# Hybrid encoder block on one core: y tiles loaded two gelus ahead, rope tables, loads and stores on other queues, PSUM pools in another order, and the out-projection by token tile

## The chip, the cores and the metric

The kernel runs on one core of one Trainium2 chip. The metric is the device time of one execution in microseconds (us). An execution is described by one profiled run: its trace has every instruction of TensorE (PE, with its weight loads PEld), VectorE (DVE), ScalarE (ACT) and GpSimd (POOL), and the DMA issues of SyncE (SP), ACT and POOL.

## What is computed

One layer of a bidirectional encoder on 256 "prompt" and 512 "sample" tokens of width 1024, all in float32. The two groups share the weights and do not see each other.

```python
h = rmsnorm(x, norm_mix_g)
u, q, k, v, qm, gl = split(h @ w_in)
# A: S5, a diagonal complex state space in both directions
y = s5_direction(u, ...) + flip(s5_direction(flip(u), ...)) + s5_d * u
z = gelu(y)
s5_out = z * sigmoid(z @ s5_w_glu)
# B: differential attention, 8 heads, two softmax maps per head
q, k = rope(rmsnorm(q, q_g)), rope(rmsnorm(k, k_g))
a = softmax(q1 k1) - lam * softmax(q2 k2)
diff_out = rmsnorm(a @ v, sub_g) * (1 - lambda_init)
# C: attention into 256 memory tokens, 4 heads
mem_out = memory_attention(qm, rmsnorm(mem, mem_norm_g), w_mem_kv, ...)
merged = sum(sigmoid(gl + b_gate)[n] * (branch[n] @ w_branch[n]) for n in 3)
x = x + merged @ w_out
h2 = rmsnorm(x, ffn_norm_g)
g, up = split(h2 @ w_gate_up)
x = x + (silu(g) * up) @ w_down
```

`lam` is exp(lq1·lk1) − exp(lq2·lk2) + a constant.

## The kernel before

**Precision.** Every float32 operand of a dense product is split into a high part (`...hi`, `wh`) and a low part (`...lo`, `wl`), and each product is three matmuls, hi·hi, hi·lo and lo·hi (`mm3`, lines 752 to 754). So nearly all PE rows of the profile have these three lines; the tile's name tells the stage.

**Weights.** `WStream` brings the weights in two pieces of 128x1024 each: an SP DMA into `wr` (line 539, three buffers), an ACT copy that makes `wh` (line 596), and `wl` by a DVE subtraction (line 602) or, with `by_dma`, by an ACT copy of the negated piece (line 599) and a POOL DMA that adds `wr` in flight (line 600). `wh` and `wl` have four buffers each. `get()` hands out a weight and prepares the next one.

**Tiles and order.** There are 768 tokens, six tiles of 128; many matmuls take them as segments of 256 and 512 (`SEGS`). The tile framework's scheduler orders the instructions of each engine; the source feeds it generators that a `Pace` object ticks at chosen rates, so that the dense matmuls of one stage are mixed with small operations of another. Each engine executes its own list in order. PSUM has eight banks, shared out by `psum(stage, d, a, b, wide)` to four kinds of tiles ("d" for dense products, "a", "b", and a double bank "w").

**Stages**, with the times of the profiled run:

- 0 to 270: memory keys, values and queries, norms, memory attention. Its output goes through `mo` tiles to `mo_scr` in DRAM.
- 270 to 628: S5. Its parameters, then the gate logits `gl` (12 weights) mixed with sixteen S5 steps. Each step ends in `psY` matmuls and an ACT copy `Ysb` (line 443) that is stored to `y_scr`; DVE's rotated input is `X` (line 390). Pools: d 2, b 4, w 1.
- 628 to 921: differential attention's projections. Pools anew: d 3, a 2, b 3. First the rope tables: twelve POOL operations (lines 1091 to 1099), and on DVE and ACT the sum and exp of `lam` (lines 1104 to 1109; the exp is line 1107). Then 72 units of 24 matmuls, 256 columns each: six `qk` units per head (ACT copy and square, lines 1125 and 1127) or six `v` units per pair of heads (ACT copy to `V`, line 1157). At units 2, 4, ..., 16 one `gelu(m)` is emitted: eight SP DMAs load a tile `y` with a reshuffle from `y_scr` (line 451), ACT squares (`yt`, line 1312) and takes tanh (line 1314), DVE does the rest (lines 1313 and 1316), SP stores `zz` to `z_scr` (line 1319). `y` has one buffer. After unit 16 (`DIFF_START`), each unit also ticks the attention `dat`: `stack` transposes q and k, copies them to `kst`/`qst` (ACT, line 1179) and swaps halves by a POOL DMA (`kst<-kst`, line 1187); `scores` does `sc` (lines 1220 and 1221), the maximum on DVE (line 1226) and exp on ACT (`p`, line 1228); then `aT`, `av` and the store of a head to `br_scr` by SP.
- 921 to 1034: branch 2 (memory), with the attention's rest ticked between its matmuls; its inputs `xm` come by 16 POOL DMAs (line 1470).
- 1034 to 1237: the GLU product with `zs` loads from `z_scr`, then branches 0 and 1. Each branch tile M loads a gate `glr` (line 1440, two buffers, SP), takes tanh on ACT (line 1441) and multiplies and adds on DVE (lines 1446 and 1449). `brr` and `x1` loads are on SP too.
- 1237 to 1305: out-projection `wo`. Pools anew: d 6, b 2. Four weights, column half c times input half kh, and for each all six token tiles (`out_rows`); the kh = 1 half adds to `x1` (line 1531).
- 1305 to 1357: row norms (`nxn`, line 793), transposes `nT` (line 781) with evacuations `fhi` and `flo` (line 746), the first gate and up products.
- 1357 to 1823: the FFN in blocks of 256 hidden columns, seven products each for gate and up instead of eight (sums of weight quarters `ws` on POOL), and `dn`, twelve tiles a block, which alternate between "b" and "d" banks and are added to x by DVE (line 1417).

Of the kernel before, what the change touches and what calls it, by code (L numbers as in the profile page):

```python
# [491 lines left out]
MEM_RATE = 1.2  # L492
DIFF_TAIL = 1.8
DIFF_RATE = 6.0 / 9.0
DIFF_START = 16
DIFF_HEADS = (0, None, 1, 2, None, 3, 4, None, 5, 6, 7, None)


# [4 lines left out]
class WStream:  # L503
# [97 lines left out]
            return  # L601
        self.sub.tensor_tensor(out=lo, in0=r, in1=hi.bitcast(F32), op=ALU.subtract)  # L602

    def ahead(self, i, parts=True):
        n = 2 * len(self.src)
        while self.n_dma < min(n, 2 * i + 3):
            self._dma()
        while parts and self.n_split < min(n, 2 * i + 2):
            self._split()
            if self.n_dma < min(n, self.n_split + 3):  # L610
                self._dma()

    def get(self):
        i = self.next
        self.next += 1
        self.ahead(i + 1)
        _, kk, cols, kind = self.src[i]
        p = self.parts.pop(i)
        if kind == "w":
            return p  # L620
        k2 = kk // 2
        at = lambda t, k, c0, n: t[:, cols * (k % k2) + c0 : cols * (k % k2) + c0 + n]
        return lambda k, c0, n: tuple(at(t, k, c0, n) for t in p[k // k2])


def hybrid_block(ctx, tc, A, outs, consts):
# [24 lines left out]

    PS, pctx = {}, [ExitStack()]

    def psum(stage, d, a, b, wide=0):
        pctx[0].close()
        pctx[0] = ctx.enter_context(ExitStack())
        for k, n in (("d", d), ("a", a), ("b", b), ("w", wide)):
            if n:
                PS[k] = pctx[0].enter_context(tc.tile_pool(name=f"ps{k}{stage}", bufs=n, space=PSUM))

    psum(0, 3, 2, 3)
    psd = lambda n="d": PS["d"].tile([128, 512], F32, name=uid(n), tag="d")
    env.psa = lambda n="a": PS["a"].tile([128, 512], F32, name=uid(n), tag="a")
    env.psb = lambda n="b": PS["b"].tile([128, 512], F32, name=uid(n), tag="b")
# [219 lines left out]
    def mem_attend():  # L884

        for h in range(4):
# [14 lines left out]
            for i in range(TILES + 2):  # L901
                if i in (3, 7):
                    sg = 0 if i == 3 else 1
                    c0, n = SEGS[sg]
                    for e in range(2):
                        mo = [k2.tile([128, 512], F32R, name=uid("mo" + w), tag="mo" + w, bufs=1) for w in "hl"]
                        ps = env.psb("mo")
                        es = slice(128 * e, 128 * e + 128)
                        for c in range(2):
                            mm3(ps[:, 0:n], vv[0][:, 2 * sg + c, es], vv[1][:, 2 * sg + c, es],  # L910
                                PT[0][:, c, 0:n], PT[1][:, c, 0:n], c == 0, c == 1)
                        split_evac(mo[0][:, 0:n], mo[1][:, 0:n], ps[:, 0:n])
                        for w in range(2):
                            nc.sync.dma_start(mo_scr[w][2 * h + e][:, c0 : c0 + n], mo[w][:, 0:n].bitcast(F32))
# [37 lines left out]
    with tc.tile_pool(name="nrm", bufs=1) as pool, tc.tile_pool(name="nrmg", bufs=1) as pg:  # L952
        xm = [load_rows(pool, ms[0])]
        gm = bcast_load(pg, A["mem_norm_g"][0], 1024, "gmem")
        xm += [load_rows(pool, ms[tt]) for tt in range(1, 4)]
        W.ahead(0, parts=False)
# [89 lines left out]

    with ExitStack() as c2:
        s5.open_work(c2)
        psum(1, 2, 0, 4, 1)
        glp = c2.enter_context(tc.tile_pool(name="glp", bufs=2))  # L1050
        pace = Pace(s5.steps(y_scr), S5_RATE)
        for c in range(12):
            W.by_dma = True
            w = W.get()
            for m in range(2):
                M = 2 * c + m
                for sg, (c0, n) in enumerate(SEGS):
                    gt = glp.tile([128, 512], F32, name=uid("glt"), tag="glt")
                    ps = psd("gl")
                    dense_fm(ps, w, m, H, c0, n)  # L1060
                    act.activation(gt[:, 0:n], ps[:, 0:n], AF.Identity, bias=bg[:, M : M + 1])
                    nc.sync.dma_start(gl_scr[M][:, c0 : c0 + n], gt[:, 0:n])
                    pace.tick(1.0 + sg)
        pace.drain()
    psum(2, 3, 2, 3)
    s5ctx.close()


# [14 lines left out]
    for i, nme in enumerate(("diff_q_g", "diff_k_g")):  # L1083
        g = rp[:, 2, 64 * i : 64 * i + 64]
        nc.sync.dma_start(g, A[nme][0].unsqueeze(0).to_broadcast([128, 64]))
        bc = lambda a: a.unsqueeze(2).to_broadcast([128, 4, 2, 32])
        cos, sin = bc(tab[:, :, 0:32]), bc(tab[:, :, 32:64])
        gb = lambda a: a.unsqueeze(1).unsqueeze(1).to_broadcast([128, 4, 2, 32])
        g1, g2 = gb(g[:, 0:32]), gb(g[:, 32:64])
        s_ = slice(2 * i, 2 * i + 2)  # L1090
        gp.tensor_tensor(out=tC[:, :, s_, 0:32], in0=cos, in1=g1, op=mul)
        gp.tensor_tensor(out=tC[:, :, s_, 32:64], in0=cos, in1=g2, op=mul)
        gp.tensor_tensor(out=tS[:, :, s_, 0:32], in0=sin, in1=g2, op=mul)
        gp.tensor_tensor(out=tS[:, :, s_, 32:64], in0=sin, in1=g1, op=mul)
        if i == 0:

            for t in (tC, tS):
                gp.tensor_scalar(out=t[:, :, s_], in0=t[:, :, s_], scalar1=0.125, scalar2=None, op0=mul)
        gp.tensor_scalar(out=tS[:, :, s_, 0:32], in0=tS[:, :, s_, 0:32], scalar1=-1.0, scalar2=None, op0=mul)
# [93 lines left out]
    def diff_attend():  # L1193
# [79 lines left out]
        def finish(h):  # L1273
            osb = X.pop(("h", h))[0]
            do = stg.tile([128, TOK], F32, name=uid("do"), tag="do", bufs=1)
            for t0, t1 in ((0, 2), (2, 6)):
                ps = env.psb("oT")
                for t in range(t0, t1):
                    pe.transpose(ps[:, 128 * (t - t0) : 128 * (t - t0) + 128], osb[:, t], env.ident)
                act.activation(do[:, 128 * t0 : 128 * t1], ps[:, 0 : 128 * (t1 - t0)], AF.Copy, scale=subg)  # L1280
            nc.sync.dma_start(br_scr[h], do)

        for i in range(N + 5):
            h, tt = divmod(i, TILES)
# [16 lines left out]
                finish(h - 1)  # L1301
            yield


    def gelu(m, pool):
        C0 = math.sqrt(2.0 / math.pi)
        y = pool.tile([128, 8, 97], F32, name=uid("y"), tag="y")
        t = pool.tile([128, 8, 97], F32, name=uid("yt"), tag="yt")
        z = stg.tile([128, TOK], F32, name=uid("zz"), tag="brr")
        s5.load_y(y, y_scr[m])  # L1310
        f = lambda a: a.rearrange("p i k -> p (i k)")
        act.activation(f(t), f(y), AF.Square)
        v.scalar_tensor_tensor(out=f(t), in0=f(t), scalar=1.0 / 0.044715, in1=f(y), op0=add, op1=mul)
# [7 lines left out]
    dat = Pace(diff_attend(), DIFF_RATE)  # L1321
    n_unit = 0
    with tc.tile_pool(name="gelu", bufs=1) as yp:
        for h in DIFF_HEADS:
            if h is not None:
                last = h
            for u_ in (v_units(last // 2) if h is None else qk_units(h)):
                n_unit += 1
                if n_unit % 2 == 0 and n_unit <= 16:
                    gelu(n_unit // 2 - 1, yp)  # L1330
                if n_unit > DIFF_START:
                    dat.tick()
    W.by_dma = False
# [30 lines left out]
    def first(what, sg, m):  # L1364


        if what not in fw:
            new_block(what, 0)
            fw[what] = W.get()
        c0, n = SEGS[sg]  # L1370
        ps = psd(what)
        dense_fm(ps, fw[what], m, F, c0, n)
# [49 lines left out]
    with ExitStack() as c5:  # L1422
# [9 lines left out]
        def branch(n_, X, first=False, MG=None, tick=lambda w: None, hook=None):  # L1432
            for c in range(4):
# [3 lines left out]
                for m in range(2):  # L1437
                    M = 2 * c + m
                    g = gtp.tile([128, TOK], F32, name=uid("glr"), tag="glr")
                    nc.sync.dma_start(g, gl_scr[8 * n_ + M])  # L1440
                    act.activation(g, g, AF.Tanh, scale=0.5)
                    for sg, (c0, n) in enumerate(SEGS):
                        ps = psd("br")
# [16 lines left out]
        def load_pair(X, src, scale=None, more=()):  # L1460
            for m in range(8):
                p = zst if m in more else stg
                r = p.tile([128, TOK], F32, name=uid("brr"), tag="brr")
                nc.sync.dma_start(r, src[m])
                split_evac(X[0][:, m], X[1][:, m], r, scale)

        Xm = pair(XA, "xm")
# [21 lines left out]
        for c in range(4):  # L1489
            w = W.get()  # L1490
            for m in range(2):
                M = 2 * c + m
                t = gtp.tile([128, TOK], F32, name=uid("gt"), tag="glr")
                zs = stg.tile([128, TOK], F32, name=uid("zs"), tag="brr")
                nc.sync.dma_start(zs, z_scr[M])
                for c0, n in SEGS:
                    ps = psd("glu")
                    dense_fm(ps, w, m, Z, c0, n)
# [75 lines left out]
    def right_factors():  # L1574

        with tc.tile_pool(name="ffb", bufs=1, side="right") as p:
# [1 line left out]
            hs = [slice(2 * j, 2 * j + 2) for j in range(2)]  # L1578

            def whole(t, b, j=slice(0, 4)):  # L1580
                v.tensor_tensor(out=t, in0=B[b][0][:, j].bitcast(F32), in1=B[b][1][:, j].bitcast(F32), op=add)
                return t

            def parts(n_):
# [84 lines left out]
```

## Time and profile before

| | us |
|---|---|
| median of 3 runs | 1828.95 (1828.82 to 1829.65) |
| the profiled execution | 1828.94 |
| its span in the trace | 1827.2 |
| PE busy (98% of the span) | 1782.8 |
| DVE busy (71%) | 1290.9 |
| ACT busy (48%) | 878.9 |
| POOL busy (14%) | 254.6 |

The mean granted clock of PE is 0.992 of full speed. In a table by windows each row is a stretch of the span: the busy time and number of instructions of PE, PEld, DVE, ACT and POOL, then the clock granted to PE, the share of the DMA engines and the GB/s. In the view of waits a row reads: engine, operation, line, what its semaphore was released by, us in total, times, longest. In a timeline a row is the start, the duration, engine, line, operation, tiles; in brackets the idle time of that engine just before, and what ended it.

### The profile page before, as it was taken

The page shows a single profiled execution, that of the slowest core. Times are in us where ns is not written, and L with a number is a line of the kernel's source. Part 1 is how long each engine was busy: PE and PEld are TensorE (multiplying, and loading weights), DVE is VectorE, ACT ScalarE, POOL GpSimd, SP SyncE. Part 2 cuts the span into 40 slices and gives each one's busy share as a digit, 9 for nine tenths or more (in the row PEclk, how much of TensorE's full clock was granted, in tenths as well). Part 3 has the DMA queues.
Part 4 walks back from the last instruction along what each step waited for, and adds up shares of the span by engine and source line. Part 5 has one row for each costly group of instructions (what it writes and reads, how often), then busy time and mean ns, then how long its engine had stood idle before and what let it go on. Part 6 is the DMA issues. An engine that isn't in the chain of part 4 may idle for free.

```text
span 1827.2 us, 29491 instructions
## 1 busy us (share of the span) xinstructions
PE 1782.8 (98%) x11286; PEld 1637.1 (90%) x11286; DVE 1290.9 (71%) x2365; ACT 878.9 (48%) x1850; POOL 254.6 (14%) x256
## 2 busy tenths in 40 slices
PE   8999999999999989999989999999999999999999
PEld 8999988899999889899978888887889999999997
DVE  6555657799999448787876535452689778787775
ACT  7444444777676346777765434222334333333331
POOL 0000000000000121110120000000024333333330
PEclk9999999999999999999999999999999999999999
DMA  9432646655655566644463445332102222222221
GB/s 266 121 100 86 125 108 148 162 136 136 151 143 151 144 146 160 162 92 100 110 191 121 161 150 184 93 111 81 58 23 93 70 70 70 70 70 70 70 70 69
DMA packets 195084, 212.07 MB, mean 116 GB/s; under 512 B 58112, under 2 KB 161792, under 8 KB 194944
## 3 DMA queue, kind: packets, MB, share of 16 engines
q1 hardware_dynamic: 183584, 172.44, 31.7%
q0 software_dynamic: 11360, 37.75, 10.3%
q8 instruction: 89, 1.46, 0.3%
q14 instruction: 51, 0.42, 0.1%
HBM read 146.11 MB, written 32.57 MB: 98 GB/s over the span
## 4 chain that ended last, share of the span: by engine, by line
PE 73%; DVE 3%; DMA 3%; SPq 2%; ACT 1%; issue 1%; POOL 0%; ACTq 0%; DVEq 0%; POOLq 0%
PE gl L752 4%; PE gl L753 4%; PE gl L754 4%; PE br L753 3%; PE br L752 3%; PE br L754 3%; PE dn L752 3%; PE dn L753 3%; PE dn L754 3%; PE gate L752 3%; PE gate L754 3%; PE gate L753 3%; PE up L752 3%; PE up L754 3%; PE up L753 3%; PE av L1257 2%
## 5 line engine op out<-in xcount | busy, mean ns | idle before, releaser
L596 ACT ACTIVATE wh<-wr 128x1024 fp32r<-128x1024 f32 x146 | 164.3, 1125 | 135.2 <-PE wo L754 30.8
L602 DVE TENSOR_TENSOR wl<-wr,wh 128x1024 fp32r<-128x1024 f32 x92 | 121.8, 1324 | 108.0 <-ACT wh L596 104.1
L1417 DVE TENSOR_TENSOR x<-x,dn 128x512 f32<-128x512 f32 x132 | 86.5, 684 | 71.1 <-PE dn L754 70.9
L752 PE MATMUL gl<-Hhi,wh 128*128 128x256 f32 (+1 forms) x384 | 133.5, 348 | 1.4 <-ACT ut L1025 1.4
L753 PE MATMUL gl<-Hlo,wh 128*128 128x256 f32 (+1 forms) x384 | 129.8, 338 | 0.0
L754 PE MATMUL gl<-Hhi,wl 128*128 128x256 f32 (+1 forms) x384 | 129.7, 338 | 0.0
L752 PE MATMUL qk<-wh,Hhi 128*128 128x256 f32 x384 | 110.0, 286 | 5.1 <-ACT V L1157 4.1
L600 POOL DMA_DIRECT2D wl<-wr x54 | 47.1, 872 | 482.4 <-ACT wl L599 443.0
L753 PE MATMUL qk<-wl,Hhi 128*128 128x256 f32 x384 | 109.5, 285 | 0.0
L754 PE MATMUL qk<-wh,Hlo 128*128 128x256 f32 x384 | 109.2, 284 | 0.0
L558 ACT ACTIVATE wh_S<-ws 128x512 fp32r<-128x512 f32 x70 | 41.7, 623 | 138.1 <-PE dn L754 110.3
L753 PE MATMUL dn<-wl,hidh 128*128 128x512 f32 x264 | 103.1, 390 | 0.0
L752 PE MATMUL dn<-wh,hidh 128*128 128x512 f32 x264 | 101.2, 391 | 0.6 <-DVE fa L1351 0.3
L754 PE MATMUL dn<-wh,hidl 128*128 128x512 f32 x264 | 98.4, 390 | 0.0
L573 POOL TENSOR_TENSOR ws<-wr,wr 128x512 f32<-128x512 f32 x20 | 31.3, 1564 | 392.2 <-PE nT L781 366.6
L752 PEld LDWEIGHTS gl<-Hhi,wh 128*128 128x128 f32 x384 | 72.3, 188 | 10.0 <-ACT ut L1025 1.8
L754 PEld LDWEIGHTS gl<-Hhi,wl 128*128 128x128 f32 x384 | 72.2, 188 | 8.7
L752 PEld LDWEIGHTS qk<-wh,Hhi 128*128 128x128 f32 x384 | 73.8, 192 | 6.1 <-ACT V L1157 4.3
L753 PEld LDWEIGHTS gl<-Hlo,wh 128*128 128x128 f32 x384 | 72.4, 188 | 7.7
L1226 DVE TENSOR_REDUCE nm<-sc 128x1 f32<-128x512 f32 (+1 forms) x96 | 56.3, 598 | 30.2 <-PE sc L1221 29.3
L754 PEld LDWEIGHTS qk<-wh,Hlo 128*128 128x128 f32 x384 | 73.9, 192 | 0.9
L753 PEld LDWEIGHTS qk<-wl,Hhi 128*128 128x128 f32 x384 | 73.9, 192 | 0.8
(449 smaller groups left out, 5974.6 us busy)
## 6 DMA issues: line engine op xcount, KB each, us to landing
wl<-wr POOLq DMA_DIRECT2D x54, 512.0 KB, 5.3
wr<-in_w_in_dram SPq DMA_DIRECT2D x48, 512.0 KB, 5.1
wr<-in_w_gate_up_dram SPq DMA_DIRECT2D x44, 512.0 KB, 3.5
wr<-in_w_branch_dram SPq DMA_DIRECT2D x24, 512.0 KB, 3.7
wr<-in_w_down_dram SPq DMA_DIRECT2D x22, 512.0 KB, 3.6
glr<-gl_scr SPq DMA_DIRECT2D x24, 384.0 KB, 3.4
wr<-in_w_mem_kv_dram SPq DMA_DIRECT2D x16, 512.0 KB, 4.8
wr<-in_w_in_dram SPq DMA_DIRECT2D x32, 256.0 KB, 3.8
```

What stands on the lines that cost most here:

```text
L558: self.nc.scalar.activation(f(hi), src, AF.Copy)
L573: gt(out=s1, in0=A21, in1=A22, op=add)
L596: self.nc.scalar.activation(hi, r, AF.Copy)
L600: self.nc.gpsimd.dma_start(lo, r.bitcast(F32R), accum_op=ALU.add)
L602: self.sub.tensor_tensor(out=lo, in0=r, in1=hi.bitcast(F32), op=ALU.subtract)
L752: pe.matmul(ps, wh, xh, start=start, stop=False)
L753: pe.matmul(ps, wh, xl, start=False, stop=False)
L754: pe.matmul(ps, wl, xh, start=False, stop=stop)
L1226: v.tensor_reduce(out=nm[:, m : m + 1], in_=ps, axis=AX.X, op=ALU.max, negate=True)
L1257: pe.matmul(po[:, 0:128], aT[:, 128 * k : 128 * k + 128], V[:, c0 // 128 + k, 128 * (h % 2) : 128 * (h % 2) + 128], start=(k == 0), stop=( ...
L1417: v.tensor_tensor(out=o, in0=o, in1=ps, op=add)
```

## The change

Eight edits in one diff; PE's instructions keep their number (10,642).

- **Gelus.** `y` gets two buffers. Two tiles are loaded ahead of the units, and each gelu then starts the load of the one after next. Gelus are emitted at every sixth unit (6, 12, ..., 48) rather than at every second up to 16. The attention is ticked from unit 14 on.
- **Rope tables.** The twelve operations go from POOL to DVE.
- **Queues.** The loads of `glr`, `brr`, `zs` and `x1` (54 DMAs) go from SP to POOL; the stores to `br_scr` (8) from SP to ACT.
- **PSUM.** The pools of a stage are opened in a chosen order of kinds: stage 1 b, w, d; stage 2 a, b, d; stage 3 d 5, b 3 (it was d 6, b 2).
- **Memory output.** The `mo` tiles get two buffers.
- **Out-projection.** For each column half both weights are held at once and the token tiles go through both, kh = 1 one tile behind kh = 0; row scales and row norms follow tile by tile.
- **Weights ahead.** `ahead` can prepare single pieces, `get` can leave it out. The first FFN weights behind the projection ("up") get `wl` by the accumulating DMA.
- **Order.** Two sums of the FFN's right factors are held in program order.

```diff
-DIFF_START = 16
+DIFF_START = 13
+GELU_UNITS = 6
...
-    def ahead(self, i, parts=True):
+    def ahead(self, i, parts=2):
...
-        while parts and self.n_split < min(n, 2 * i + 2):
+        while parts and self.n_split < min(n, 2 * i + parts):
...
-    def get(self):
+    def get(self, ahead=True):
...
-        self.ahead(i + 1)
+        if ahead:
+            self.ahead(i + 1)
...
-    psum(0, 3, 2, 3)
+    psum(0, d=3, a=2, b=3)
...
-                        mo = [k2.tile([128, 512], F32R, name=uid("mo" + w), tag="mo" + w, bufs=1) for w in "hl"]
+                        mo = [k2.tile([128, 512], F32R, name=uid("mo" + w), tag="mo" + w) for w in "hl"]
...
-        psum(1, 2, 0, 4, 1)
+        psum(1, b=4, w=1, d=2)
...
-    psum(2, 3, 2, 3)
+    psum(2, a=2, b=3, d=3)
...
-        gp.tensor_tensor(out=tC[:, :, s_, 0:32], in0=cos, in1=g1, op=mul)
+        v.tensor_tensor(out=tC[:, :, s_, 0:32], in0=cos, in1=g1, op=mul)
...
-            nc.sync.dma_start(br_scr[h], do)
+            act.dma_start(br_scr[h], do)
...
+    ys = {}
+
+    def gelu_load(m, pool):
+        if m < 8:
+            ys[m] = pool.tile([128, 8, 97], F32, name=uid("y"), tag="y", bufs=2)
+            s5.load_y(ys[m], y_scr[m])
...
     def gelu(m, pool):
...
-        y = pool.tile([128, 8, 97], F32, name=uid("y"), tag="y")
+        y = ys.pop(m)
...
-        s5.load_y(y, y_scr[m])
...
+        for m in range(2):
+            gelu_load(m, yp)
         for h in DIFF_HEADS:
...
-                if n_unit % 2 == 0 and n_unit <= 16:
-                    gelu(n_unit // 2 - 1, yp)
+                m, r = divmod(n_unit, GELU_UNITS)
+                if r == 0 and 1 <= m <= 8:
+                    gelu(m - 1, yp)
+                    gelu_load(m + 1, yp)
...
-                    nc.sync.dma_start(g, gl_scr[8 * n_ + M])
+                    gp.dma_start(g, gl_scr[8 * n_ + M])
...
-                nc.sync.dma_start(r, src[m])
+                gp.dma_start(r, src[m])
...
-                nc.sync.dma_start(zs, z_scr[M])
+                gp.dma_start(zs, z_scr[M])
...
-            nc.sync.dma_start(x1[t], xs[t])
+            gp.dma_start(x1[t], xs[t])
...
-        psum(3, 6, 0, 2)
+        psum(3, d=5, b=3)
...
-        for c, kh in ((0, 0), (0, 1), (1, 0)):
-            w = W.get()
-            for tt in range(TILES):
-                out_rows(w, c, kh, tt)
-
-        w = W.get()
-        for tt in range(TILES):
-            out_rows(w, 1, 1, tt)
-            if tt % 2:
-                row_scales(tt - 1)
-            if tt > 2:
-                rows(tt - 3)
+        for c in range(2):
+            w = [W.get(False)]
+            W.ahead(W.next)
+            w.append(W.get(False))
+            for t in range(TILES + 1):
+                if t < TILES:
+                    out_rows(w[0], c, 0, t)
+                if t == TILES - 1:
+                    W.ahead(W.next)
+                if t:
+                    out_rows(w[1], c, 1, t - 1)
+                    if c and t % 2 == 0:
+                        row_scales(t - 2)
+                if c and t in (4, 5):
+                    rows(t - 4)
+        rows(2)
+        rows(3)
+        W.by_dma = True
         first("gate", 0, 0)
-        rows(3)
+        W.ahead(W.next, 1)
         first("gate", 0, 1)
         rows(4)
+        W.ahead(W.next)
         rows(5)
...
+                if b in ("B11", "B12"):
+
+                    tc.keep_in_program_order(i)
...
+    W.by_dma = False
     factors = right_factors()
```

More of the change, by code (lines that the diff above doesn't have):

```diff
@@ L652, in hybrid_block, with psum @@
     PS, pctx = {}, [ExitStack()]
-    def psum(stage, d, a, b, wide=0):
+    def psum(stage, **kinds):
         pctx[0].close()
         pctx[0] = ctx.enter_context(ExitStack())
-        for k, n in (("d", d), ("a", a), ("b", b), ("w", wide)):
-            if n:
-                PS[k] = pctx[0].enter_context(tc.tile_pool(name=f"ps{k}{stage}", bufs=n, space=PSUM))
-    psum(0, 3, 2, 3)
+        for k, n in kinds.items():
+            PS[k] = pctx[0].enter_context(tc.tile_pool(name=f"ps{k}{stage}", bufs=n, space=PSUM))
+    psum(0, d=3, a=2, b=3)
     psd = lambda n="d": PS["d"].tile([128, 512], F32, name=uid(n), tag="d")
@@ L955, in hybrid_block @@
         xm += [load_rows(pool, ms[tt]) for tt in range(1, 4)]
-        W.ahead(0, parts=False)
+        W.ahead(0, 0)
         nc.sync.dma_start(gk, A["mem_k_g"][0].unsqueeze(0).to_broadcast([128, 256]))
@@ L1090, in hybrid_block @@
         s_ = slice(2 * i, 2 * i + 2)
-        gp.tensor_tensor(out=tC[:, :, s_, 0:32], in0=cos, in1=g1, op=mul)
-        gp.tensor_tensor(out=tC[:, :, s_, 32:64], in0=cos, in1=g2, op=mul)
-        gp.tensor_tensor(out=tS[:, :, s_, 0:32], in0=sin, in1=g2, op=mul)
-        gp.tensor_tensor(out=tS[:, :, s_, 32:64], in0=sin, in1=g1, op=mul)
+        v.tensor_tensor(out=tC[:, :, s_, 0:32], in0=cos, in1=g1, op=mul)
+        v.tensor_tensor(out=tC[:, :, s_, 32:64], in0=cos, in1=g2, op=mul)
+        v.tensor_tensor(out=tS[:, :, s_, 0:32], in0=sin, in1=g2, op=mul)
+        v.tensor_tensor(out=tS[:, :, s_, 32:64], in0=sin, in1=g1, op=mul)
         if i == 0:
             for t in (tC, tS):
-                gp.tensor_scalar(out=t[:, :, s_], in0=t[:, :, s_], scalar1=0.125, scalar2=None, op0=mul)
-        gp.tensor_scalar(out=tS[:, :, s_, 0:32], in0=tS[:, :, s_, 0:32], scalar1=-1.0, scalar2=None, op0=mul)
+                v.tensor_scalar(out=t[:, :, s_], in0=t[:, :, s_], scalar1=0.125, scalar2=None, op0=mul)
+        v.tensor_scalar(out=tS[:, :, s_, 0:32], in0=tS[:, :, s_, 0:32], scalar1=-1.0, scalar2=None, op0=mul)
     nc.sync.dma_start(subg, A["diff_sub_g"][0].unsqueeze(1))
@@ L1368, in first @@
             new_block(what, 0)
-            fw[what] = W.get()
+            fw[what] = W.get(what == "up")
         c0, n = SEGS[sg]
@@ L1580, in whole @@
             def whole(t, b, j=slice(0, 4)):
-                v.tensor_tensor(out=t, in0=B[b][0][:, j].bitcast(F32), in1=B[b][1][:, j].bitcast(F32), op=add)
+                i = v.tensor_tensor(out=t, in0=B[b][0][:, j].bitcast(F32), in1=B[b][1][:, j].bitcast(F32), op=add)
+                if b in ("B11", "B12"):
+                    tc.keep_in_program_order(i)
                 return t
```

## The prediction, made before the changed kernel was run

> **What bounds the kernel now.** I read the engines' busy time first, then the windows, then TensorE's (PE's) waits, then ScalarE's (ACT's) timeline around the worst of them.
>
> ```profile
> span 1827.2 us, 29491 instructions
> PE 1782.8 (98%) x11286; PEld 1637.1 (90%) x11286; DVE 1290.9 (71%) x2365; ACT 878.9 (48%) x1850; POOL 254.6 (14%) x256
> ```
>
> PE is the bound: 1827.2 − 1782.8 = 44.4 us without a matmul. No matmul is removed (10,642 PE instructions in either program), so only these 44.4 us and matmuls at a lowered clock can be won. The windows say where (columns: busy us and count of PE, its weight loads, DVE, ACT, POOL; granted clock; DMA):
>
> ```profile
> 630.00:675.00 45.00, 38.31 (x323) 37.69 (x321) 19.38 (x37) 17.53 (x32) 13.60 (x15) 1.00 0.60 144
> 675.00:720.00 45.00, 42.23 (x334) 42.03 (x335) 30.16 (x70) 26.93 (x58) 5.45 (x7) 0.92 0.74 170
> 720.00:765.00 45.00, 40.78 (x320) 39.68 (x319) 31.90 (x63) 32.68 (x84) 3.73 (x5) 0.96 0.55 147
> 765.00:900.00 135.00, 135.00 (x1112) 132.46 (x1111) 115.21 (x311) 102.24 (x285) 14.05 (x19) 1.00 0.45 104
> 1305.00:1350.00 45.00, 40.97 (x240) 36.08 (x239) 41.59 (x64) 19.06 (x33) 5.14 (x3) 0.96 0.08 24
> 1350.00:1800.00 450.00, 449.64 (x2366) 420.08 (x2365) 359.62 (x498) 147.16 (x256) 164.79 (x114) 1.00 0.22 68
> ```
>
> Three windows from 630 to 765, where the qk/v units run with the gelus, lack 13.7 us of PE, and the clock costs 45 × 0.08 + 45 × 0.04 = 5.4 us more. From 765 to 900 and from 1350 to 1800 nothing is left to win. PE's waits (what, for what: us in total, times, longest) name what came last:
>
> ```profile
> PE sc L1220 <- ACT p L1228: 8.6, 7, 4.2
> PE qk L752 <- ACT V L1157: 4.1, 1, 4.1
> PE nT L781 <- DVE flo L746: 3.9, 3, 2.7
> ...
> PE sc L1220 <- DMA kst<-kst: 2.5, 1, 2.5
> PE v L752 <- ACT V L1157: 2.5, 1, 2.5
> ```
>
> Behind V and p stands one cause. ACT works in order, and the gelu's first operation waits on it for its tile y:
>
> ```profile
> 673.13 0.85 ACT L1312 ACTIVATE yt<-y 128x776 f32<-128x776 f32 x1 [7.09 <-DMA y<-y_scr]
> 673.89 1.04 ACT L599 ACTIVATE wl<-wr 128x1024 fp32r<-128x1024 f32 x1
> 674.84 0.36 ACT L1157 ACTIVATE V<-v 128x256 f32<-128x256 f32 x1
> ```
>
> V's evacuation, ready long before, runs 1.7 us after yt started; meanwhile the three "d" banks fill and PE stands 4.14 us at 675.25. On SP's queue the eight y loads of this gelu were issued from 664.94 to 670.49, after the store of the previous zz (664.42). The same picture stands at 658.47 (ACT idle 7.47, PE then 2.47), 699.41 (3.83; the copies to kst come late, their transfer takes 701.03 to 705.05, and sc waits 2.52) and 744.83 (5.17; p late, sc 4.22).
>
> **The change, part by part.** All against the profiled execution: span 1827.2 us, 1.7 us around it, 1828.9 us in all, which is the median of the runs shown (1828.95).
>
> *End of S5.* PE stands 1.47 us at 624.83 (psY waits for DVE's X) and 0.63 at 628.16 (the first qk waits for the evacuation that frees its bank). In the changed program's order 21 qk matmuls stand ahead of psY's last 11: 21 × 0.117 = 2.45 us of work, in banks that nothing late holds. Both stalls fit under it: **−2.1**, between −2.1 and 0.
>
> *Rope tables on DVE.* POOL's twelve operations last from 637.26 to 648.25, 11.0 us. By DVE's rows of these sizes (0.41 us for 128x256, 0.68 for 128x512) they are 10 × 0.41 + 2 × 0.68 = 5.5 us. DVE is idle there (8.99 us before 633.76, 6.68 before 640.87), but its in-order queue now puts them ahead of lam's reduction, for which ACT's exp (L1107) waits; that ran at 641.97 and I place it near 644. ACT's qk evacuations stand behind it, PE has three banks, and the stall of 0.34 at 642.77 may grow. None if four units are evacuated first, as the order has it; 3 if exp comes a whole unit (24 × 0.117 = 2.8 us) later. I take the middle, **+1.5** (0 to 3).
>
> *Gelus.* y has two buffers and is loaded two gelus ahead. The source puts a gelu at every sixth unit; the scheduler's order puts the yt's behind about units 4, 6, 9, 12, 15, 16, 18, 21. A load begins when the gelu two earlier is through, 3 to 4 units, 8.4 to 11.2 us, before it is used; by before's rows a load takes 7 to 10 us from the zz store to yt (647.79 to 658.47, 664.42 to 673.13). So most waits go, but not where two gelus stand close. Walking ACT's order by these rows: yt2 waits about 4.4 us with banks free, yt3 0.8, yt5 3.3, the others nearly nothing. yt5 again delays a copy to kst and its 4.0 us transfer, for which I charge 2.4 us of PE (0 to 4). With 0.7 for yt3, 3.1 us of stalls stay of 13.7. For the clock: the matmuls after 705.1 ran at a pitch of 0.213 us instead of 0.117 up to 709.1, after a stall of 2.52, and none did after 2.47 at 659.64 (window clock 1.00). So a stall of 2.4 has an even chance of a dip of 1.8 us: 0.9. **Gain 19.1 − 4.0 = −15.1**, between −19 and −9 (half of the waits stay).
>
> [...]
>
> *DIFF_START.* The heads' attend steps begin three units earlier. No matmul is added. DVE is busy 196.7 of 270 us from 630 to 900, so with 5.5 us more in some 255 us it has 79%: 0.
>
> *Loads moved.* 54 loads go from SP to POOL, whose issues cost 0.54 to 0.87 us each by its rows, on an engine that is idle from 1000 to 1300.
>
> ```profile
> wl<-wr POOLq DMA_DIRECT2D x54, 512.0 KB, 5.3
> ...
> glr<-gl_scr SPq DMA_DIRECT2D x24, 384.0 KB, 3.4
> ...
> xmhi<-mo_scrh POOLq DMA_DIRECT2D x8, 384.0 KB, 9.2
> ```
>
> A glr tile takes 3.4 us to land from SP; the nearest POOL rows are 5.3 and, sixteen at once, 9.2. Two buffers and an 8.45 us period (SP issues at 1154.47 and 1162.91) give 16.9 us for landing, tanh (0.85) and DVE's four operations (2 × 0.69 + 2 × 0.42 = 2.2): up to 13.8 us of landing costs nothing lasting. 0, between −1 and +2. The br_scr stores on ACT (eight issues of some 0.35) and the second mo buffer lie where PE does not wait: 0.
>
> *Banks apart.* At 1237.45 wo waits 0.87 us; the profile names the weight copy, but the bank is br's, read by DVE from 1236.61 to 1237.30. In after it has another: **−0.9** (−0.9 to 0).
>
> *Projection tile by tile.* The 288 wo matmuls already run at 0.234 us. What can go is what follows: nT's waits of 2.69, 0.98 and 0.28 us (DVE is at 41.6 of 45: row norms, nT evacuations, weight subtractions together) and the clock's 0.04 × 45 = 1.8. Row scales start earlier and two subtractions become accumulating DMAs on POOL (5.3 us to land); the first "up" half then lands, worked forward, about 18 us after the last wo, and PE needs it at about 17. Both halves now fill all four weight buffers, so each next weight is split within the last two row groups: 2 × 12 × 0.234 = 5.6 us, against 2 × 1.1 (ACT) + 1.3 (DVE): fits. Recoverable 5.7, of which I take **−3.0** (−5.7 to +2).
>
> *FFN.* At peak; the "d" banks fall from 6 to 5: 0 (below, a rival).
>
> **Sum:** −2.1 + 1.5 − 15.1 − 0.9 − 3.0 = −19.6: 1828.9 − 19.6 = **1809.3 us**.
>
> **Rivals.**
>
> *A, the forecast (0.55):* 1809, own range 1803 to 1815.
>
> *B, the spread does not spread (0.22).* The gelus cluster at 15, 16, 18, 21 and each load is behind a weight load on SP that waits for the accumulating DMA; half of 19.1 stays, the stalls move to kst. For it: two y loads are issued behind such a weight load. Against: yt had no load in hand before and has one now. Price +5.5 to +9: 1815 to 1818, say 1817.
>
> *C, all stalls of the touched stages go (0.10):* −2.1 − 19.1 − 0.9 − 5.7 = −27.8: 1801.
>
> *D, the other side (0.05): the FFN waits for banks.* Each of its ten blocks (45.5 us) has 12 dn tiles, 16.8 us of PE, evacuated by DVE with 12 × 0.684 = 8.2 us. Five banks are 7.0 us of dn, six were 8.4. It decides where DVE's other work in a dn stretch exceeds 16.8 − 8.2 + 7.0 = 15.6 us: beyond that every us is paid ten times, and 2.4 us more per block undoes the gain: 1833. Against: in the block at 1456 to 1473 DVE was idle 6.8 us waiting for dn.
>
> *E, the gain is given back (0.06):* DVE, with rope and attend earlier, delays sc and the projection's start by what the gelus free; 1827.
>
> *F, POOL's loads starve (0.02).* If a glr takes 17 us to land, 24 tiles lose (17 − 13.8)/2 = 1.6 us each, 38 us: 1848. Against: no POOL row is over 9.2. [...]
>
> **Numbers.** A measurement of this kernel tells about 0.2% (3.7 us) from no change. Faster: A + B + C = 0.87; same: E, 0.06; slower: D + F, 0.07. The range leaves out D, E, F and the outer parts of C and B: 1800 to 1822.
>
> **What would show it.** In after: no PE gap near 622 to 626 (S5's end); no idle over 5 us before L1312 and PE at 42 or more of 45 in each window from 630 to 765; no PE gap at the first wo; nT's waits at flo under 2 us; 1350 to 1800 shifted but full. I am wrong by the gelus if PE still waits for V, kst or p by over 5 us before the gelus end; by rope if PE waits over 3 us for the first qk evacuations; by the banks if dn waits for x.

## The result, and the profile after

The changed kernel takes 1806.91 us (median; 1805.94 to 1807.31), the kernel before 1829.3 beside it: a ratio of 0.9876, 95% interval 0.9859 to 0.9894. The forecast was 1809.3, its range 1800 to 1822. The profiled execution took 1807.31, its span is 1805.5.

The first lines of the page, and the windows of the changed kernel (columns as before the change):

```profile
span 1805.5 us, 29484 instructions
...
PE 1773.6 (98%) x11286; PEld 1629.6 (90%) x11286; DVE 1287.0 (71%) x2375; ACT 881.7 (49%) x1852; POOL 278.9 (15%) x300
```

```profile
630.00:675.00 45.00, 41.57 (x348) 41.19 (x348) 31.59 (x65) 25.18 (x46) 3.45 (x4) 0.98 0.79 186
675.00:720.00 45.00, 43.50 (x350) 42.39 (x350) 38.82 (x86) 31.93 (x73) 7.54 (x12) 0.98 0.76 195
720.00:765.00 45.00, 45.00 (x372) 44.08 (x372) 35.83 (x94) 35.94 (x101) 4.98 (x7) 1.00 0.49 117
...
900.00:945.00 45.00, 37.45 (x211) 30.37 (x210) 32.45 (x80) 25.26 (x73) 12.44 (x24) 0.92 0.64 200
```

PE is idle for 1805.5 − 1773.6 = 31.9 us instead of 44.4; its busy time fell by 9.2 us with the same matmuls (11,286 in either trace; the 10,642 of the prediction stands in none), and the mean clock rose from 0.992 to 0.997, which is 0.005 × 1800 = 9 us. The three windows from 630 to 765 lack 4.9 us instead of 13.7. The window from 900 to 945 has 37.5 us of PE and a clock of 0.92. The changed kernel gets to its first br 20 us earlier, so the window of before that belongs beside it is 920 to 965: 38.7 us of PE and a clock of 1.00.

The waits of PE in the changed kernel:

```profile
PE qkT L1177 <- DVE qst L1187: 3.9, 2, 2.9
PE mv L756 <- ACT kr L847: 3.3, 2, 2.0
...
PE br L757 <- DMA xmlo<-mo_scrl: 1.7, 3, 0.8
...
PE sc L1224 <- ACT p L1232: 1.6, 2, 0.9
PE sc L1224 <- DMA kst<-kst: 1.5, 3, 0.7
...
PE br L756 <- DMA xmhi<-mo_scrh: 1.3, 4, 0.6
```

V and p are gone as the long waits. In their place stand qkT's wait for DVE's qst and br's waits for the loads of xm. The wait of mv lies in the first 35 us; it is 1.0 us in before, but 3.5 with the mo buffer alone, so it varies without an edit at that place.

A table by stages is surer than a sum of waits, because each stage but the third and fourth holds nearly the same matmuls in both kernels. Each row is the time from one landmark of PE to the next, in the profiled executions; the last column is what the prediction gave for it.

| from, to | before | after | change | predicted |
|---|---|---|---|---|
| start to the last u | 307.0 | 301.4 | −5.6 | 0 |
| to the last gl | 313.1 | 311.7 | −1.4 | 0 |
| to the first br (branch 2) | 305.6 | 292.5 | −13.1 | −15.7 |
| to the first glu | 108.4 | 113.2 | +4.7 | 0 |
| to the first wo | 203.3 | 201.0 | −2.3 | −0.9 |
| to dn of block 1 | 173.6 | 169.9 | −3.7 | −3.0 |
| to the last dn | 411.8 | 411.6 | −0.2 | 0 |
| sum | | | −21.6 | −19.6 |

So the total is nearly right and the parts are not: two gains that I had put at nothing, and one loss, stand beside the terms of the sum. The third and fourth row share the attention, and what is done earlier in one is missing in the other; together they took 414.0 us before and take 405.6 now, a gain of 8.4 where the prediction had 15.7.

### The profile page after: what moved, and what is told of

Same layout as the page of the kernel before. It is cut to its first block, busy times and chain, and to the rows that moved or that the text cites. A ratio compares the mean times of both kernels' runs of the same rounds, so it can differ in the third digit from the quotient of the medians.

```text
span 1805.5 us, 29484 instructions
## 1 busy us (share of the span) xinstructions
PE 1773.6 (98%) x11286; PEld 1629.6 (90%) x11286; DVE 1287.0 (71%) x2375; ACT 881.7 (49%) x1852; POOL 278.9 (15%) x300
## 3 DMA queue, kind: packets, MB, share of 16 engines
q8 instruction: 89, 1.46, 0.3%
## 4 chain that ended last, share of the span: by engine, by line
PE 56%; DVE 5%; DMA 4%; ACT 2%; issue 1%; SPq 1%; POOL 0%; ACTq 0%; DVEq 0%; POOLq 0%
PE br L757 4%; PE br L758 4%; PE br L756 4%; PE dn L756 3%; PE dn L757 3%; PE dn L758 3%; PE gate L756 3%; PE gate L757 3%; PE gate L758 3%; PE up L756 3%; PE up L758 3%; PE up L757 3%; PE av L1261 2%; PE qk L758 2%; PE qk L757 2%; PE qk L756 2%
## 5 line engine op out<-in xcount | busy, mean ns | idle before, releaser
L757 PE MATMUL qk<-wl,Hhi 128*128 128x256 f32 x384 | 108.7, 283 | 0.0
L1230 DVE TENSOR_REDUCE nm<-sc 128x1 f32<-128x512 f32 (+1 forms) x96 | 56.8, 597 | 22.5 <-PE sc L1225 21.6
L1232 ACT ACTIVATE p<-sc,nm 128x512 f32<-128x512 f32 (+1 forms) x96 | 59.0, 618 | 24.6 <-DVE nm L1230 20.1
```

Of the source, the lines that this page charges most:

```text
L757: pe.matmul(ps, wh, xl, start=False, stop=False)
L1230: v.tensor_reduce(out=nm[:, m : m + 1], in_=ps, axis=AX.X, op=ALU.max, negate=True)
L1232: act.activation(pm[:, 0:n], ps, AF.Exp, bias=nm[:, m : m + 1], accum_out=s1s[:, tt : tt + 1] if m == 0 else s2)
```

## The experiments

Twelve kernels, each timed against the kernel before on its chip. Differences from the changed kernel are taken from the ratios, times 1829.3 us.

| run | median | ratio to before, 95% |
|---|---|---|
| changed kernel | 1806.91 | 0.9876 (0.9859 to 0.9894) |
| e1_mo_alone | 1822.96 | 0.9969 (0.9958 to 0.998) |
| e2_gelus_old | 1814.1 | 0.9919 (0.9906 to 0.9933) |
| e3_start16 | 1806.89 | 0.9878 (0.9864 to 0.9891) |
| e4_rope_pool | 1805.78 | 0.9873 (0.986 to 0.9887) |
| e5_loads_sp | 1807.5 | 0.9873 (0.986 to 0.9886) |
| e6_projection_old | 1811.1 | 0.9894 (0.9879 to 0.9908) |
| e7_banks_old | 1806.41 | 0.9866 (0.9852 to 0.9881) |
| e8_gelus_alone | 1824.65 | 0.9972 (0.9962 to 0.9983) |
| e10_rate_up | 1806.8 | 0.987 (0.9855 to 0.9885) |
| e11_kst_act | 1803.91 | 0.9854 (0.9838 to 0.9871) |
| e12_kst_act_rope_pool | 1798.29 | 0.9824 (0.981 to 0.9839) |
| e13_bank2_old | 1804.61 | 0.9858 (0.9844 to 0.9873) |

### The second mo buffer, alone on the kernel before

```diff
-mo = [k2.tile([128, 512], F32R, name=uid("mo" + w), tag="mo" + w, bufs=1) for w in "hl"]
+mo = [k2.tile([128, 512], F32R, name=uid("mo" + w), tag="mo" + w) for w in "hl"]
```

> The kernel before with one edit, two buffers for the mo tiles. Theory: in before, ACT's copy into the single mo tile waits for its store to mo_scr (6.28 us before 225.80), the next mqh copy stands behind it, and PE's qss waits 3.44 us at 232.66, with a clock of 0.91 and 0.94 behind it; by the two traces the stage up to the first b matmul is 5.6 us shorter in the changed kernel. So 5.6 us less than before, about 1823.5. Rival (the prediction's reading): the mo stores delay only ACT, and the 5.6 us come from elsewhere: 1829, within 0.5 us.

1822.96: 0.0031 × 1829 = 5.7 us less, so the theory holds. The wait of PE in before, which this run no longer has:

```profile
PE qss L895 <- DVE mqsq L881: 3.4, 1, 3.4
```

ACT's timeline of before, and then of this run, at the same place:

```profile
225.80 0.60 ACT L745 ACTIVATE moh<-mo 128x512 fp32r<-128x512 f32 x1 [6.28 <-DMA mo_scrh<-moh]
226.29 2.31 ACT L596 ACTIVATE wh<-wr 128x1024 fp32r<-128x1024 f32 x1
228.38 0.65 ACT L745 ACTIVATE mqh<-mq 128x512 fp32r<-128x512 f32 x1
```

```profile
220.78 2.44 ACT L596 ACTIVATE wh<-wr 128x1024 fp32r<-128x1024 f32 x1 [0.51 <-PE mq L753]
222.90 0.75 ACT L745 ACTIVATE mqh<-mq 128x512 fp32r<-128x512 f32 x1
```

With one mo tile, moh waits for its store, and the weight copy and mqh stand behind it in ACT's order; mqh comes 5.5 us later. From it DVE makes mql and mqsq, for which PE's qss waits. PE's windows, before and then with two buffers:

```profile
215.00:235.00 20.00, 16.56 (x87) 14.27 (x86) 7.69 (x10) 7.47 (x8) 0.00 (x0) 0.91 0.99 198
235.00:262.00 27.00, 27.00 (x173) 24.79 (x173) 14.72 (x42) 11.31 (x20) 0.36 (x6) 0.94 0.40 92
```

```profile
215.00:235.00 20.00, 20.00 (x123) 17.78 (x122) 10.28 (x23) 8.22 (x9) 0.00 (x0) 1.00 1.03 205
235.00:262.00 27.00, 27.00 (x165) 23.84 (x165) 12.47 (x29) 12.99 (x20) 0.36 (x6) 1.00 0.37 89
```

3.4 us of stall and 0.09 × 20 + 0.06 × 27 = 3.4 us of clock at most: that is the 5.6 us, part of the low clock falling into the stall itself.

### The gelus, taken out of the changed kernel and put alone on the kernel before

```diff
-        y = ys.pop(m)
+        y = pool.tile([128, 8, 97], F32, name=uid("y"), tag="y")
...
+        s5.load_y(y, y_scr[m])
...
-                m, r = divmod(n_unit, GELU_UNITS)
-                if r == 0 and 1 <= m <= 8:
-                    gelu(m - 1, yp)
-                    gelu_load(m + 1, yp)
+                if n_unit % 2 == 0 and n_unit <= 16:
+                    gelu(n_unit // 2 - 1, yp)
```

> The changed kernel with the gelus as before: one y buffer, each loaded by its own gelu, at units 2 to 16; the start of the attention stays at 13. Theory: most of the 13 us won from the end of S5 to the first branch matmul is the gelus', so 9 to 13 us more than the changed kernel, 1816 to 1820. Rival: with rope on DVE, the banks apart and the attention three units earlier, little waits for the gelus, and the time rises by under 4 us, to 1811 at most.

The other run is the same edit in reverse on the kernel before.

> The kernel before with one edit: two y buffers, loads two gelus ahead, gelus at every sixth unit; the attention starts after unit 16. Taken from the changed kernel this edit cost 7.2 us. Theory: the y waits in before also cause the clock's dips and the kst stall, so alone it wins more, near the prediction's 15: 11 to 15 us, 1814 to 1818. Rival: the gain is 7 in either kernel, since other waits (kst, qst, p) come up in their place: 1821 to 1823.

Without the gelus' edit the changed kernel is 0.0043 × 1829 = 7.9 us slower: less than the theory's 9 to 13, more than the rival's 4. Alone the edit wins 0.0028 × 1829 = 5.1 us: not the 11 to 15 of the theory, and a little less than the rival's 7. So it is worth some 5 to 8 us in either company. Why not 15 shows in ACT's timeline of the changed kernel, where the gelus' first operation still waits:

```profile
652.09 0.85 ACT L1322 ACTIVATE yt<-y 128x776 f32<-128x776 f32 x1 [5.15 <-DMA wr<-in_w_in_dram]
...
661.81 0.86 ACT L1322 ACTIVATE yt<-y 128x776 f32<-128x776 f32 x1 [2.64 <-DMA y<-y_scr]
...
669.98 0.85 ACT L1322 ACTIVATE yt<-y 128x776 f32<-128x776 f32 x1 [3.34 <-DMA wr<-in_w_in_dram]
670.85 0.86 ACT L1183 ACTIVATE qst<-qkT 64x256 fp32r<-64x256 f32 x2
```

The longest wait is 5.15 us and no longer 7.47, but there are five over 2 us, where before had four, since the scheduler puts the gelus closer than every sixth unit. The one at 669.98 holds back the qst copies, so that PE's qkT stands 2.88 us at 672.43. That is a wait in the place of V's. In the run with the gelus alone, the stretch to the first br is 305.6 − 300.3 = 5.3 us shorter and branch 2 is 113.4 − 108.4 = 5.0 us longer in the profiled execution: the loss of branch 2 that the changed kernel shows too. That execution took 1827.04, more than this kernel's median, so its stages show less than the 5.1 us. In the changed kernel with the old gelus the two stages take 413.4 us together instead of 405.6, 7.8 us more, in accord with the 7.9.

### The attention's start, and how much of it is done before branch 2

```diff
-DIFF_START = 13
+DIFF_START = 16
```

> The changed kernel with the attention starting after unit 16 again. Theory: the earlier start pulls attention work forward, so that less of it is left to cover the loads of xm at the head of branch 2, where the changed kernel loses 4.7 us against before (clock 0.92 from 900 to 945); with 16 these come back, and the wait of qkT for qst at 672 (2.9 us) goes: 3 to 7 us faster than the changed kernel, 1800 to 1804. Rival: the loss at branch 2 is the xm loads' own rate and the end of the attention chain, whatever the start: 1806 to 1808.

The time is the changed kernel's (1806.89). The rival's time came out, but not its reason: branch 2 did get 113.2 − 108.2 = 5.0 us shorter, as the theory had it, and the stage before got 297.4 − 292.5 = 4.9 us longer, with kst arriving late (PE waits 2.65 and 1.80 us for it at 694.7 and 699.6). The three units only move a loss. In this run br's gaps in branch 2 come to 0.6 us, where the changed kernel has 3.0 and before 0.8. That less attention is left to cover the loads of xm is not the reason, by the next run:

```diff
-DIFF_RATE = 6.0 / 9.0
+DIFF_RATE = 0.72
```

> The changed kernel with DIFF_RATE 0.72 instead of 0.667: more of the attention is done before branch 2, while PE's order keeps a row of 36 attention matmuls with no br matmul between them (38 in the changed kernel). Theory: branch 2 loses time because of this row, whose sc, aT and qkT each wait for ACT or DVE; then branch 2 still loses 8 to 10 us in stalls over 0.1 us, and the time is 1805 to 1809. Rival: too little attention is left to cover the xm loads; then less attention in branch 2 makes it worse by 2 us or more: 1809 or above.

At the first br 236 of 816 attention matmuls are left, 252 in the changed kernel. Branch 2 keeps its stalls: the gaps over 0.1 us come to 6.7 us by the trace (6.4 in the changed kernel), less than the 8 to 10 of the theory. The time is 1806.8, as the theory has it, and the rival's 1809 is out: the amount is not the cause.

### The row of attention matmuls in branch 2

In the changed kernel's trace 42 attention matmuls (the expectations count 38) stand in a row on PE, from 929.4 to 943.0, with no br between them, 13.7 us. Before has such a row too (50). PE's timeline of the changed kernel in it:

```profile
930.87 0.38 PE L1224 MATMUL sc<-kst,qst 128*128 128x256 f32 x1 [0.88 <-ACT p L1232]
...
932.74 0.65 PE L1224 MATMUL sc<-kst,qst 128*128 128x512 f32 x1 [0.67 <-ACT p L1232]
...
938.20 0.44 PE L1177 MATMUL qkT<-ident,rope 128*128 128x128 f32 x2 [0.64 <-ACT aT L1249]
939.63 1.04 PE L1177 MATMUL qkT<-ident,rope 128*128 128x128 f32 x4 [0.99 <-DVE qst L1187]
```

The windows of this stretch, in the changed kernel and then in before, where the row ran from 946 to 958:

```profile
930.00:935.00 5.00, 3.46 (x13) 2.52 (x14) 4.54 (x14) 2.31 (x8) 0.00 (x0) 0.79 0.00 0
935.00:940.00 5.00, 3.37 (x17) 2.67 (x16) 3.75 (x8) 4.61 (x15) 0.00 (x0) 0.84 0.01 3
940.00:945.00 5.00, 5.00 (x21) 4.18 (x20) 4.88 (x11) 3.00 (x9) 2.83 (x6) 0.68 0.53 168
```

```profile
945.00:950.00 5.00, 3.46 (x25) 2.80 (x23) 2.55 (x13) 2.33 (x10) 0.00 (x0) 1.00 0.01 3
950.00:955.00 5.00, 3.81 (x22) 2.93 (x23) 4.72 (x15) 4.39 (x15) 0.00 (x0) 1.00 0.00 0
955.00:960.00 5.00, 4.60 (x23) 3.24 (x22) 4.84 (x14) 3.69 (x11) 0.51 (x1) 1.00 0.56 162
```

PE stands about as much in either, so the row is not what the changed kernel lost by; the run with the attention's start at 16 has the row of before (50) too, and its branch 2 takes 108.2 us. Two things are new in this execution: the clock, (0.21 + 0.16 + 0.32) × 5 = 3.5 us at most, and the head of the branch, where br waits for xm (3.0 us in the seven gaps of the changed kernel, 0.8 in before). The loss does not need the clock: the run with the old out-projection, shown further below, has PE's matmuls of branch 2 in the changed kernel's order and the full clock in all of it, and still takes 112.2 us. Its waits for xm there:

```profile
PE br L757 <- DMA xmlo<-mo_scrl: 2.4, 4, 1.1
...
PE br L756 <- DMA xmhi<-mo_scrh: 0.9, 3, 0.5
```

These are 3.3 us against 0.7 in before, where branch 2 took 108.4. So br's waits for xm are the larger part of what comes with the order. Why the loads come later in it, no run here shows.

An order without the row came from another queue for the swap of kst's halves:

```diff
-                gp.dma_start(T[m][o], T[m][s])
+                act.dma_start(T[m][o].bitcast(F32), T[m][s].bitcast(F32))
```

> The changed kernel with the kst half swaps issued by ACT instead of POOL, where they stand behind the 16 xm loads. In the order that comes out, br matmuls stand between all groups of attention matmuls (the longest row is 16 instead of 38). Theory (the row costs it): branch 2 gets 5 to 7 us shorter, the stage before stays within 2 us: 1800 to 1803. Rival: the xm loads fill the DMA engines from 905 to 925 and set branch 2's length in any order: 1805 to 1808.

1803.91, 0.0022 × 1829 = 4.0 us less by the ratios and 3.0 by the medians: between the two bands, with intervals that overlap the changed kernel's. Branch 2 fell to 108.7, its attention waits are gone, but br now waits 1.54, 1.39 and 1.49 us for xm: the loads are a second cause, which the theory lacked. In the profiled execution the stage before is 3.0 us longer; its stretches of lowered clock there cost 5.1 us, where the changed kernel's cost 1.7.

With the rope tables moved as well:

```diff
-        v.tensor_tensor(out=tC[:, :, s_, 0:32], in0=cos, in1=g1, op=mul)
+        gp.tensor_tensor(out=tC[:, :, s_, 0:32], in0=cos, in1=g1, op=mul)
...
-                gp.dma_start(T[m][o], T[m][s])
+                act.dma_start(T[m][o].bitcast(F32), T[m][s].bitcast(F32))
```

> The same, and the rope tables on POOL as before. Theory: both gains add, 1.1 us from the rope tables and 5 from the row: 1799 to 1802, faster than both kernels. Rival: as with kst on ACT alone, 1805 to 1808.

1798.29, faster than both kernels, by 0.0052 × 1829 = 9.5 us than the changed one (intervals 0.981 to 0.9839 and 0.9859 to 0.9894), a little more than the theory gave. Branch 2 takes 105.3 us and the stage before 290.6. Two edits that win little alone (1.1 us at most and 3.0 to 4.0, both inside the intervals) win 9.5 together. In this run's windows from 630 to 765 the clock stays at 1.00. The clock is a small part of it: its mean over the four executions is 0.997 in either kernel, and 0.996 with the swaps on ACT alone, a difference of some 2 us. What else makes the two edits worth more together, no run here shows.

### The banks

```diff
-        psum(1, b=4, w=1, d=2)
+        psum(1, d=2, b=4, w=1)
...
-    psum(2, a=2, b=3, d=3)
+    psum(2, d=3, a=2, b=3)
```

> The changed kernel with the pools of stages 1 and 2 opened in the order of before (d first). Theory: the bank order is what took away 1.40 us at the first gl matmul, and lets the qk matmuls go ahead of the last psY (2.1 us at 624.83 and 628.16): 2.5 to 4 us slower than the changed kernel, 1809.5 to 1811. Rival: the scheduler finds other banks or another order that hide it, 1806 to 1808.

All three stalls come back at the sizes of before (1.40 at the first gl, 1.46 at psY, 0.63 at the first qk), and the time is 1806.41, as with the rival: the theory's mechanism is right and its sum is not. The stretch to the first br gets 8.8 us longer and branch 2 11.5 us shorter (101.7), since this order has no row and does 18 more attention matmuls earlier. A fourth stall returns as well: wo waits 0.87 us again at 1218.74, though stage 3 keeps its new pools.

And stage 2 alone:

```diff
-    psum(2, a=2, b=3, d=3)
+    psum(2, d=3, a=2, b=3)
```

> The changed kernel with the pools of stage 2 alone in the order of before (d, a, b); stage 1 keeps b, w, d. The order has no long row of attention matmuls in branch 2. Theory: the two stalls at the end of S5 (1.46 and 0.63 us) come back, the one at the first gl matmul (1.40) does not, and branch 2 is 9 to 11 us shorter while the stage before is as much longer: 1805 to 1807, as with both stages' order undone, less 1.4: 1804.5 to 1806. Rival: the bank order of stage 2 is worth its 2.1 us and nothing comes back: 1808 to 1810.

1804.61: as the theory has it, the stage before is 10.5 us longer and branch 2 12.9 shorter (100.2). wo waits its 0.87 us again too, so it is the order of stage 2 that took that stall away. The bank order of stage 2 wins these 3.0 us and pays them back in branch 2: with the order of before the two stages take 403.2 us together, in the changed kernel 405.6.

### The rope tables, the loads, the projection

The rope tables back on POOL, all twelve operations in this way:

```diff
-        v.tensor_tensor(out=tC[:, :, s_, 0:32], in0=cos, in1=g1, op=mul)
+        gp.tensor_tensor(out=tC[:, :, s_, 0:32], in0=cos, in1=g1, op=mul)
```

> The changed kernel with the rope tables on POOL again. Theory (the prediction's step): on DVE they delay lam's exp and cost 1.5 us of PE at the first units (the changed kernel's gaps of 1.05 at 628.3 and 0.55 at 643.1); on POOL these go: 1805.4. Rival: on POOL the tables take 11 us instead of 5.5, the first rope of a head and the accumulating DMAs on POOL's queue come later, and the time rises by 1 to 4 us: 1808 to 1811.

1805.78: 1.1 us less by the medians and 0.0003 × 1829 = 0.5 by the ratios, but the intervals overlap, so this run can't tell it from nothing. The rival's 1808 is out. Of the two gaps that the theory names, only the one of 0.55 us at 643.1 is gone; the other stays, with 1.36 us at 630.14, so the rope tables on DVE did not make it.

The loads on SP again, and the br_scr stores too:

```diff
-                    gp.dma_start(g, gl_scr[8 * n_ + M])
+                    nc.sync.dma_start(g, gl_scr[8 * n_ + M])
...
-            act.dma_start(br_scr[h], do)
+            nc.sync.dma_start(br_scr[h], do)
```

> The changed kernel with the 54 loads (glr, brr, zs, x1) and the 8 stores to br_scr on SP again. Theory (the prediction's step): the queue doesn't matter, 1805.5 to 1808. Rival: on SP a gate's load stands behind weight loads that wait, the gap of 0.98 us at the head of branch 0 comes back (the changed kernel has none), and the weights come later in places: 1808 to 1811.

1807.5, ratio 0.9873: the queue doesn't matter. The gap at the head of branch 0 stays away on SP, so POOL is not what removed it; it is missing in both runs with a single edit on the kernel before, too.

The out-projection as before (four weights one after the other, no accumulating DMAs for up):

```diff
-        for c in range(2):
-            w = [W.get(False)]
...
+        for c, kh in ((0, 0), (0, 1), (1, 0)):
+            w = W.get()
+            for tt in range(TILES):
+                out_rows(w, c, kh, tt)
```

> The changed kernel with the out-projection, the row norms and the first gate and up weights in the order of before (pools d 5 and b 3 stay). Theory: from the first wo to the second FFN block the changed kernel won 3.7 us, and all of it comes from this part: 1810 to 1811. Rival: the banks set apart won it, nT's waits do not come back: 1806 to 1808.

1811.1: by the ratio 0.0018 × 1829 = 3.3 us, by the medians 4.2; in the profiled executions 174.2 us instead of 169.9 from the first wo to block 1, with a wait of nT of 1.90 us that the changed kernel hasn't, and 1.7 us of lowered clock. The intervals overlap, but every execution of this run is slower than every one of the changed kernel. The theory fits.

## Why the prediction was right or wrong

*End of S5 (−2.1).* Right as a step: both stalls are gone, and each comes back at its size with the old bank order. As a gain in the total it does not show, since the same bank order changes the attention's order and costs as much in branch 2. I had counted the order of the matmuls around it and not what follows.

*Rope (+1.5).* Not confirmed: 0.5 to 1.1 us by the experiment, which can't be told from nothing. The mechanism accounts for one gap of 0.55 us. lam's exp came at 636.21, 23.1 us after the last gl, where before had 21.9: it moved by 1.2 us, not by 2, and with the tables on POOL again it came 22.7 us after.

*Gelus (−15.1).* The failed step. The mechanism is shown (y's loads hold ACT, and V, qst, kst and p behind it), but the size is 5 to 8 us. I let most of the y waits go to nothing; five idle times of 2.3 to 5.2 us before yt stayed. Two of the signs in the prediction came out against it, though barely: 5.15 us of idle before yt, where none over 5 was to stay, and 41.6 us of PE in the first of the three windows, where 42 was the least. And I counted each stall as gone with its cause, where others followed: with the old gelus in the changed kernel PE's longest waits there are for qst (4.14 us), aT (1.89) and p (2.58), not for V, and the three windows lack 10.8 us of PE instead of 13.7.

*mo (0).* Wrong: 5.7 us. "The second mo buffer lies where PE does not wait" was read off the engine that the wait names (DVE's mqsq) instead of followed back: mqsq waits for mqh on ACT, and mqh stood behind moh's wait of 6.28 us.

*DIFF_START (0).* Right in the total (1806.89 with 16), though it moves 5 us from one stage to the next.

*Loads (0).* Right, and rival F did not come: glr lands in 3.4 us from POOL as it did from SP, with DVE at 71%.

*Banks (−0.9 and 0).* Right: wo's 0.87 is gone, and it comes back with stage 2's old order, as the prediction's reading (the bank is br's) has it. The first gl's 1.40 us at 308.81, the same kind of stall, I had not priced.

*Projection (−3.0).* Right: −3.7 in the trace up to block 1, 3.3 to 4.2 by the experiment.

*FFN (0) and rival D.* Nearly right. From block 1 on it takes 411.6 us after 411.8. But from the first dn to the last it takes 495.7 after 493.8: dn waits 1.01 us for DVE's x at 1347.18, which was the prediction's sign against its banks, and up waits 1.01 for ACT's fs at 1370.78. Both stand in every run made from the changed kernel, with the old projection too, and in neither made from the kernel before. They come once, not ten times as in rival D; which edit makes them is not separated. They lie ahead of block 1, so that the row with −3.7 has them in it.

*Branch 2 (not in the sum).* The 4.7 us lost were foreseen by no rival. Rival E (the gain is given back) is the nearest, but at a place that it doesn't name.

So the total was right by luck: gains of 5.6 and 1.4 us that had no price nearly cancel the gelus' shortfall and a loss of 4.7 us that had none either.

## What to carry to other kernels

Follow a wait back past the engine that the profile names to the first in-order queue with a long idle time in front of something unrelated; a store that holds a single buffer is such a place, and one more buffer was worth as much as the rewritten gelus. Don't add up stalls of one stretch as if each went with its cause, because the next waits stand right behind them: take one out and time it. Where a scheduler sets the order, read the new order of the stages after the edit, too: a bank order that wins 2 us there can lose them 300 us later.

## What the runs showed of the hardware

The clock also fell without a long stop of PE. In the changed kernel it was 0.79, 0.84 and 0.68 in three windows of 5 us from 930 to 945, with no gap over 1.12 us since 900; in before, windows with the same share of PE (3.46 and 3.81 of 5) stayed at 1.00.

Shorter windows tell more. They are 3.41 us long, as long as the clock stood at 0.50 from 932.93 to 936.34. The first four are from the changed kernel, the last four from before:

```profile
929.52:932.93 3.41, 1.86 (x10) 1.06 (x9) 3.10 (x10) 1.59 (x6) 0.00 (x0) 1.00 0.00 0
932.93:936.34 3.41, 3.41 (x15) 3.07 (x15) 1.92 (x7) 2.06 (x7) 0.00 (x0) 0.50 0.00 0
936.34:939.75 3.41, 1.77 (x10) 1.08 (x9) 3.22 (x7) 3.02 (x9) 0.00 (x0) 1.00 0.02 5
939.75:943.16 3.41, 3.41 (x13) 2.95 (x14) 3.35 (x7) 2.66 (x9) 2.18 (x5) 0.50 0.26 52
...
658.01:661.42 3.41, 1.78 (x15) 1.78 (x16) 1.97 (x5) 2.19 (x5) 0.00 (x0) 1.00 0.74 224
661.42:664.83 3.41, 3.41 (x32) 3.41 (x31) 3.41 (x6) 1.51 (x4) 0.00 (x0) 1.00 0.02 5
...
702.39:705.80 3.41, 0.89 (x8) 0.71 (x7) 3.38 (x6) 1.55 (x5) 0.53 (x1) 1.00 0.23 51
705.80:709.21 3.41, 3.41 (x19) 3.41 (x18) 3.41 (x5) 0.66 (x2) 0.00 (x0) 0.50 0.69 192
```

The prediction's puzzle stands in the last four: the stretch with the stall of 2.52 us had PE busy for 0.89 of 3.41 us, and the next ran at 0.50; the one in which the stall of 2.47 ended had 1.78, and the next ran at 1.00. In the changed kernel stretches with 1.86 and 1.77 were followed by 0.50. So neither the longest stall nor PE's share of the stretch tells by itself when the clock falls. What decides it, no run here shows. The mean clock differs between executions of one kernel, too: 0.994 to 0.999 in the four with the swaps on ACT and the rope tables on POOL.
